# Conditioning in 32-column groups of TensorE, and the sample tokens' convolution as products on GpSimd

## The chip, the cores and the metric

The kernel runs on one core of one Trainium2 chip. The time is that of one execution on the device, in microseconds (us). A core has TensorE (PE, matrix products into PSUM; PEld is its loading of weights), VectorE (DVE), ScalarE (ACT), GpSimd (POOL), SyncE (SP, which here issues every DMA), 16 DMA engines, SBUF with 128 partitions as working memory, and PSUM with eight banks of 128 x 512 f32.

## The reference

One layer of a streaming encoder for two groups of requests with the same weights: a prompt of 1024 tokens and 8 samples of 16 tokens, 1152 tokens of width 1024. All is f32.

```python
sh1, sc1, gt1, sh2, sc2, gt2, sh3, sc3, gt3 = split(silu(c) @ w_ada + b_ada, 9)   # 9 rows c: prompt, 8 samples
x = x + 0.5 * gt1 * swiglu(rms(x) * (1 + sc1) + sh1, w_up1, w_down1)              # first FFN, 2816 wide
z = (rms(x) * (1 + sc2) + sh2) @ w_in            # q, k, v, forget logits, and a pair a, gt for the convolution
o = forgetting_attention(q, k, v, logf)          # 8 heads of 64; samples also see 256 cached rows
u = a * sigmoid(gt)                              # 512 channels, 30 earlier rows in front of each sequence
y = silu(layernorm(depthwise_conv31(u) + conv_b))
x = x + gt2 * (concat(o, y) @ w_out)
x = rms(x + 0.5 * gt3 * swiglu(rms(x) * (1 + sc3) + sh3, w_up2, w_down2))         # second FFN
```

The outputs are x of both groups and the new states (k, v, logf, the last 30 rows of u). What matters here: the conditioning, `silu(c) @ w_ada`, is 9 rows by 1024 by 9216 columns (a weight of 36 MB that is read once); and the convolution gives, for each of 512 channels, 1024 prompt tokens and 8 x 16 sample tokens, a sum of 31 products.

## The kernel before, in words

The 1152 tokens stand in SBUF transposed, in three chunks of 384 columns (c = 0, 1, 2; the samples are the last 128 columns of chunk 2). Large products are made from fp32r parts: each operand is split into hi and lo, and three fp32r matmuls (hi by hi, hi by lo, lo by hi: `mm3`, L478 to L480) stand for one f32 product. Weights come in blocks of 512 KB (`raw`); ScalarE casts them to hi (`wh`, L117) and GpSimd subtracts lo (`wl`, L118), four blocks deep.

The order of TensorE's instructions is that of the program (a manual schedule up to the attention). The other engines' instructions are placed by a scheduler with its own estimates. Work that is woven into TensorE's stream hangs on ticks: `defer(n, f)` runs f at the n-th tick from now, and each half of an up-projection (24 matmuls) and each half of a down-projection ticks once.

The conditioning is cut into 18 groups j of 512 columns, with 8 blocks k of 128 rows each. The first two groups (scale and shift of the first half of the first norm) are full f32 matmuls with 9 columns of stationary data (L348). The others are split: `ahi` on ScalarE (L335), `alo` on VectorE or GpSimd (L336), and two fp32r matmuls (L351, L352) whose 18 stationary columns hold the hi and lo parts of silu(c). Groups 1 and 2 stand ahead of the first FFN, groups 3 and 4 within its first unit, at once; the other 14 are woven into the first FFN, one block a tick (two blocks a tick for the first 20 or so). At a group's end `ada_tail` copies the sum (`ev`), transposes it in four pieces (`pt`), adds the bias into `mods` and makes what the norms and gates use. The blocks of the first four groups come by two loads of 256 KB (`araw`) and one of 1.5 MB (`abulk`) each, the others by one load of 256 KB a block with three buffers.

After the first FFN comes the projection: first the columns of the convolution's pair (`glu`, four tiles ct of 128 channels; `ua` and `ub`), then six column blocks cb of q, k, v (`z`, L872 to L874), nine token tiles each. The convolution runs on VectorE beside it (`conv_taps`): for each ct and each of 31 taps j one operation over 1024 prompt tokens, summed in PSUM (`cv`, L728), and one over the 128 sample tokens, summed in SBUF (`acc`, L729). `run(conv, n)` issues n taps. The attention follows; its first loads (`kp` and others) go into memory that the projection frees. Then the output projection, the second FFN and the final norm.

Of the kernel before, what the change touches and what calls it, by code (L numbers as in the profile page):

```python
# [1 line left out]

# [6 lines left out]
F32 = mybir.dt.float32  # L9
# [34 lines left out]
def trunk_layer(  # L44
# [84 lines left out]
    def kpn(ap):  # L129
        return ap.rearrange("(k p) n -> p k n", p=P)  # L130
# [56 lines left out]
    cst = const.tile([P, KD, 18], F32R, name="cst")  # L187
# [31 lines left out]
    cst32 = pro.tile([P, KD, 9], F32, tag="cst32", name="cst32")  # L219
    xin = {}  # L220

    def load_x(i):
# [78 lines left out]
    KORD = [6, 7, 0, 1, 2, 3, 4, 5]  # L301

    def ada_load(n):
        if n < 18 * KD and n not in ada_raw:
            j, k = ADA_ORDER[n // KD], KORD[n % KD]
            t = adp.tile([P, 512], F32, tag="araw", name="araw", bufs=3)
            sp.dma_start(t, w_ada[0, k * P:(k + 1) * P, j * 512:(j + 1) * 512])
            ada_raw[n] = t

    def ada_bulk(g, tag):  # L310
        j = ADA_ORDER[g]
        for n in range(g * KD, g * KD + 2):
            ada_load(n)
        t = hp.tile([P, 6, 512], F32, tag=tag, name="abulk")
        sp.dma_start(t, kpn(w_ada[0, :6 * P, j * 512:(j + 1) * 512]))
        for k in range(6):
            ada_raw[g * KD + 2 + k] = t[:, k]

    FULL = 2
    NA = 18 * KD  # L320
    ada_q, ada_t, ada_n, ada_p = [], [], [0], [None]

    def ada_split():
        n = ada_n[0]
        ada_n[0] += 1
        if n >= 4 * KD - 2:
            for q in range(max(n, 4 * KD), n + 3):
                ada_load(q)
        raw = ada_raw.pop(n)
        if n < FULL * KD:  # L330
            ada_q.append((n, raw, None))
            return
# [6 lines left out]
    def ada_mm():  # L339
        n, hi, lo = ada_q.pop(0)  # L340
        j, k = ADA_ORDER[n // KD], KORD[n % KD]
        first, last = n % KD == 0, n % KD == KD - 1
        if first:
            ada_p[0] = bank("pa")
        pa = ada_p[0]
        if lo is None:
            r = 9
            pe.matmul(pa[:r, :], lhsT=cst32[:, k, :], rhs=hi, start=first, stop=last)  # L348
        else:
            r = 18  # L350
            pe.matmul(pa[:r, :], lhsT=cst[:, k, :], rhs=hi, start=first, stop=False)  # L351
            pe.matmul(pa[:r, :], lhsT=cst[:, k, :], rhs=lo, start=False, stop=last)  # L352
        if last:
            ev = tmp(512, "ev", r)
            act.copy(ev, pa[:r, :])
            ada_t.append((j, r, ev))

    def ada_tail():
        j, r, ev = ada_t.pop(0)
# [3 lines left out]
        ptv = pt[:, :4 * r].rearrange("p (i s) -> p i s", s=r)  # L363
        dst = mods[:, 4 * j:4 * j + 4, :]
        dve.tensor_tensor(
            dst, ptv[:, :, 0:9], bada[:, 4 * j:4 * j + 4].unsqueeze(2).to_broadcast([P, 4, 9]), ALU.add)
        if r == 18:
            dve.tensor_tensor(dst, ptv[:, :, 9:18], dst, ALU.add)
        finish_mod(j)

    def ada_step():
        if ada_t:
            ada_tail()
        if ada_n[0] < NA:
            ada_split()
            if len(ada_q) > 2:
                ada_mm()
        elif ada_q:
            ada_mm()
        return ada_n[0] < NA or ada_q or ada_t  # L380

    def ada_blocks(n):
        for _ in range(n):
            ada_split()
            if len(ada_q) > 1:
                ada_mm()

    def ada_close():
        while ada_q:
            ada_mm()  # L390
        ada_tail()

    def ada_group():
        ada_blocks(KD)
        while ada_q:
            ada_mm()

    def run(gen, n):
# [204 lines left out]
    ada_tail()  # L603
    ada_group()
    stats_c(0)
    ada_tail()
    ws.split(2)
    ada_bulk(2, "hh2")
    ada_bulk(3, "hl2")
    ws.limit = b_out  # L610

    def chain(c, i):
# [8 lines left out]
    def first(k):  # L621
        if k == 0:
            norm_apply(0, 0, (0, 1))
        elif k == 1:
            for i in range(3, 6):
                place_x(i, xin[i])
        elif k == 4:
            ada_blocks(KD + 2)
            ada_tail()
            ada_blocks(KD - 2)  # L630
            ada_close()
# [84 lines left out]

    def conv_taps():
        for ct in range(4):
            av = acc[ct][:, SEQ:].rearrange("p (s t) -> p s t", t=TS)
            cv = ps.tile([P, SEQ], F32, tag="cv", name="cv", bufs=1)  # L720
            for j in range(CW):
                w = cw[:, ct, j:j + 1]
                u0, u1 = u[ct][:, j:j + SEQ], usv[ct][:, :, j:j + TS]
                if j == 0:
                    dve.tensor_scalar(cv, u0, w, convb[:, ct:ct + 1], ALU.mult, ALU.add)
                    dve.tensor_scalar(av, u1, w, convb[:, ct:ct + 1], ALU.mult, ALU.add)
                else:
                    dve.scalar_tensor_tensor(cv if j < CW - 1 else acc[ct][:, :SEQ], u0, w, cv, ALU.mult, ALU.add)  # L728
                    dve.scalar_tensor_tensor(av, u1, w, av, ALU.mult, ALU.add)  # L729
                yield  # L730

    conv = conv_taps()

    def glu(ct, c, w0, w1):
        pa, pb = glu_mm(c, w0, w1)
# [125 lines left out]
    for cb, (c0, n) in enumerate(QKV):  # L861
# [3 lines left out]
        for tt in [8] + list(range(8)):  # L865
# [18 lines left out]
            else:  # L884
# [30 lines left out]

# [474 lines left out]
```

## Time and profile before

| | us |
|---|---|
| median of 3 runs | 2399.08 (2397.36 to 2401.82) |
| the profiled execution | 2399.03 |
| its span, first to last instruction | 2397.3 |
| PE busy in the span | 2335.4 (97%) |
| DVE busy | 1277.2 (53%) |
| ACT busy | 729.5 (30%) |
| POOL busy | 680.8 (28%) |
| granted TensorE clock, mean | 0.989 |

A row of the page's groups gives line, engine, operation, the tiles written and read, shapes and count; then the busy time, the mean of one in ns, and the idle time of the engine ahead of it with what ended it. A row of the timeline gives the start in us from the span's start, the duration, and the instructions that are merged in it (x4). Matmuls overlap and their ends are modelled, so what one costs is read from start to start. An f32 matmul leaves two records, one for each pass.

### The profile page before, as it was taken

What the parts mean: (1) busy time and instruction counts of PE and PEld (TensorE: products, weight loads), DVE (VectorE), ACT (ScalarE), POOL (GpSimd) and SP (SyncE); (2) the same over time, 40 slices, a digit from 0 to 9 for tenths busy, and PEclk for the clock granted to TensorE, in tenths of its full rate; (3) what the DMA queues carried; (4) which work ended last, traced back from release to release, by engine and by line L of the source; (5) the groups of instructions that cost most, each with busy time, mean ns of one, the idle gap of its engine ahead of it and who ended that gap; (6) DMA issues with size and microseconds to landing.
All of it is one profiled execution on the core that took longest, in us unless ns stands there. A gap on an engine that the chain in (4) does not pass through costs nothing.

```text
span 2397.3 us, 34979 instructions
## 1 busy us (share of the span) xinstructions
PE 2335.4 (97%) x13971; PEld 2236.0 (93%) x13971; DVE 1277.2 (53%) x2381; ACT 729.5 (30%) x1567; POOL 680.8 (28%) x535
## 2 busy tenths in 40 slices
PE   8899999999999999999989999999999999999998
PEld 4899999999999999999987779999999999999997
DVE  5542543343344436799978887744442344333345
ACT  5533222222111113412658764431111111111112
POOL 2254444443211211131536651112112121121220
PEclk9899999999999999999999999999999999999999
DMA  8133333332111111114233331111111111111102
GB/s 296 57 115 96 95 94 99 93 89 66 45 44 36 47 42 36 37 54 140 89 94 126 93 96 36 45 36 51 38 36 53 36 45 44 36 53 36 37 26 79
DMA packets 176699, 165.81 MB, mean 69 GB/s; under 512 B 11135, under 2 KB 143147, under 8 KB 176529
## 3 DMA queue, kind: packets, MB, share of 16 engines
q1 hardware_dynamic: 176537, 163.58, 22.5%
q8 instruction: 110, 1.80, 0.3%
q14 instruction: 52, 0.43, 0.1%
HBM read 147.10 MB, written 16.68 MB: 68 GB/s over the span
## 4 chain that ended last, share of the span: by engine, by line
PE 84%; DVE 10%; ACT 2%; DMA 2%; issue 1%; POOL 0%; SPq 0%; DVEq 0%; ACTq 0%; POOLq 0%
PE ub L479 8%; PE ub L478 8%; PE ub L480 8%; PE ua L479 8%; PE ua L480 8%; PE ua L478 8%; PE d L480 8%; PE d L478 8%; PE d L479 8%; DVE cv L728 4%; DVE acc L729 1%; DMA nfb<-nfd 1%; PE pa L351 1%; PE pa L352 1%; PE wo L480 1%
## 5 line engine op out<-in xcount | busy, mean ns | idle before, releaser
L118 POOL TENSOR_TENSOR wl<-raw,wh 128x1024 fp32r<-128x1024 f32 (+1 forms) x152 | 368.5, 2432 | 1246.3 <-ACT wh L117 1237.9
L517 DVE TENSOR_TENSOR g<-ub,sg 128x384 f32<-128x384 f32 x132 | 73.6, 558 | 764.5 <-PE ub L480 735.8
L478 PE MATMUL ub<-hh,wh 128*128 128x384 f32 x1168 | 397.7, 341 | 2.5 <-ACT hh L462 2.5
L479 PE MATMUL ub<-hl,wh 128*128 128x384 f32 x1168 | 397.5, 340 | 1.9 <-DVE hl L463 1.9
L480 PE MATMUL ub<-hh,wl 128*128 128x384 f32 x1168 | 397.0, 340 | 0.0
L478 PE MATMUL ua<-hh,wh 128*128 128x384 f32 x1136 | 382.0, 336 | 3.7 <-ACT hh L473 3.3
L479 PE MATMUL ua<-hl,wh 128*128 128x384 f32 x1136 | 381.7, 336 | 0.2
L480 PE MATMUL ua<-hh,wl 128*128 128x384 f32 x1136 | 381.3, 336 | 0.0
L485 DVE SCALAR_TENSOR_TENSOR x<-d,hgate,x 128x384 f32<-128x384 f32 (+1 forms) x528 | 296.1, 571 | 134.0 <-PE d L480 127.9
L117 ACT CAST wh<-raw 128x1024 fp32r<-128x1024 f32 (+1 forms) x160 | 165.6, 1050 | 652.4 <-issue 332.6
L478 PE MATMUL d<-gh,wh 128*128 128x384 f32 x1056 | 357.7, 339 | 3.7 <-DVE t L461 3.6
L480 PE MATMUL d<-gh,wl 128*128 128x384 f32 x1056 | 358.1, 339 | 0.0
L479 PE MATMUL d<-gl,wh 128*128 128x384 f32 x1056 | 357.3, 338 | 0.0
L478 PEld LDWEIGHTS ub<-hh,wh 128*128 128x128 f32 x1168 | 221.2, 189 | 7.6 <-ACT hh L462 2.7
L479 PEld LDWEIGHTS ub<-hl,wh 128*128 128x128 f32 x1168 | 221.2, 189 | 4.3 <-DVE hl L463 2.7
L478 PEld LDWEIGHTS ua<-hh,wh 128*128 128x128 f32 x1136 | 214.4, 189 | 9.5 <-ACT hh L473 4.4
L480 PEld LDWEIGHTS ub<-hh,wl 128*128 128x128 f32 x1168 | 221.2, 189 | 0.0
L479 PEld LDWEIGHTS ua<-hl,wh 128*128 128x128 f32 x1136 | 214.3, 189 | 2.9 <-DVE hl L474 1.0
L336 POOL TENSOR_TENSOR alo<-araw,ahi 128x512 fp32r<-128x512 f32 x112 | 149.0, 1335 | 237.2 <-ACT ahi L335 237.2
L480 PEld LDWEIGHTS ua<-hh,wl 128*128 128x128 f32 x1136 | 214.4, 189 | 0.0
L478 PEld LDWEIGHTS d<-gh,wh 128*128 128x128 f32 x1056 | 199.4, 189 | 8.8 <-DVE t L461 3.9
L521 DVE TENSOR_TENSOR gl<-g,gh 128x384 fp32r<-128x384 f32 x132 | 164.6, 1247 | 68.8 <-ACT gh L520 68.8
(274 smaller groups left out, 3634.8 us busy)
## 6 DMA issues: line engine op xcount, KB each, us to landing
raw<-in_w_up_dram SPq DMA_DIRECT2D x88, 512.0 KB
araw<-in_w_ada_dram SPq DMA_DIRECT2D x120, 256.0 KB
raw<-in_w_down_dram SPq DMA_DIRECT2D x44, 512.0 KB
raw<-in_w_in_dram SPq DMA_DIRECT2D x18, 512.0 KB
abulk<-in_w_ada_dram SPq DMA_DIRECT2D x4, 1536.0 KB
out_dram<-yo SPq DMA_DIRECT2D x18, 256.0 KB
out_dram<-qkv SPq DMA_DIRECT2D x34, 128.0 KB
room<-in_cache_k_dram SPq DMA_DIRECT2D x8, 512.0 KB
```

What stands on the lines that cost most here:

```text
L117: act.copy(hi[:, :a * b], raw)
L118: self.sub.tensor_sub(lo[:, :a * b], raw, r32(hi[:, :a * b]))
L336: (pool_e if n >= 4 * KD else dve).tensor_sub(lo, raw, r32(hi))
L351: pe.matmul(pa[:r, :], lhsT=cst[:, k, :], rhs=hi, start=first, stop=False)
L352: pe.matmul(pa[:r, :], lhsT=cst[:, k, :], rhs=lo, start=False, stop=last)
L478: pe.matmul(out, lhsT=wh, rhs=mh_, start=first, stop=False)
L479: pe.matmul(out, lhsT=wh, rhs=ml_, start=False, stop=False)
L480: pe.matmul(out, lhsT=wl, rhs=mh_, start=False, stop=last)
L485: dve.scalar_tensor_tensor(xs[:, :n], b[:, :n], gate[:, dt, 0:1], xs[:, :n], ALU.mult, ALU.add)
L517: dve.tensor_tensor(g32, pb[:, :C], sg, ALU.mult)
L521: dve.tensor_sub(gl[:, cs], g32, r32(gh[:, cs]))
L728: dve.scalar_tensor_tensor(cv if j < CW - 1 else acc[ct][:, :SEQ], u0, w, cv, ALU.mult, ALU.add)
```

## The change

Conditioning. The 18 groups are put into six sets, three of two groups and three of four. silu(c) stands in `cst32`, 9 columns padded with zeros to 32. For each block k of a set, one f32 matmul for each of its groups goes to partitions 32i to 32i + 31 of one PSUM bank `pa` that is kept for it (the rotating banks are seven instead of eight). Splits and their buffers are gone. Blocks of the later sets come as 128 x 2048 (or 128 x 1024) tiles with two buffers; each load is asked for behind the step two earlier. Set 1 stands ahead of the first FFN, set 2 in its first unit; the third set has a step a tick, the others a step every fourth tick. One tail serves a set.

Convolution. `conv_taps` does the prompt tokens alone. `conv_sample` makes, for a channel tile and two samples, all 2 x 16 x 31 products in one GpSimd operation that reads overlapping windows of u and the 31 taps, into a stretch of `acc[3]`, and VectorE sums each 31 in one operation; the bias is added by GpSimd. The one buffer `wn` is shared by all 16 rounds.

```diff
-    nb = 8
+    nb = 7
...
-    act.copy(cst[:, :, 0:9], pcv)
-    dve.tensor_copy(cst32, pcv)
-    dve.tensor_sub(cst[:, :, 9:18], pcv, r32(cst[:, :, 0:9]))
+    dve.memset(cst32, 0.0)
+    dve.tensor_copy(cst32[:, :, 0:9], pcv)
...
-    ADA_ORDER = [2, 0, 3, 1, 4, 5] + list(range(6, 18))
+    SETS = [[2, 0], [3, 1], [4, 5]] + [list(range(j, j + 4)) for j in range(6, 18, 4)]
+    KORD = [6, 7, 0, 1, 2, 3, 4, 5]
+    STEPS = [(s, k) for s in range(len(SETS)) for k in KORD]
...
+        t = adp.tile([P, 2048], F32, tag="araw", name="araw", bufs=2)
+        rows = w_ada[0, k * P:(k + 1) * P]
+        if js == list(range(js[0], js[0] + len(js))):
+            sp.dma_start(t[:, :512 * len(js)], rows[:, 512 * js[0]:512 * (js[-1] + 1)])
+        else:
+            for i, j in enumerate(js):
+                sp.dma_start(t[:, 512 * i:512 * (i + 1)], rows[:, 512 * j:512 * (j + 1)])
...
-        hi = adp.tile([P, 512], F32R, tag="ahi", name="ahi", bufs=3)
-        lo = adp.tile([P, 512], F32R, tag="alo", name="alo", bufs=3)
-        act.copy(hi, raw)
-        (pool_e if n >= 4 * KD else dve).tensor_sub(lo, raw, r32(hi))
-        ada_q.append((n, hi, lo))
...
     def ada_mm():
...
         if first:
-            ada_p[0] = bank("pa")
+            ada_p[0] = ps.tile([P, 512], F32, tag="pa", name="pa", bufs=1)
         pa = ada_p[0]
-        if lo is None:
-            r = 9
-            pe.matmul(pa[:r, :], lhsT=cst32[:, k, :], rhs=hi, start=first, stop=last)
-        else:
-            r = 18
-            pe.matmul(pa[:r, :], lhsT=cst[:, k, :], rhs=hi, start=first, stop=False)
-            pe.matmul(pa[:r, :], lhsT=cst[:, k, :], rhs=lo, start=False, stop=last)
+        for i, raw in enumerate(ada_raw.pop(n)):
+            pe.matmul(pa[32 * i:32 * i + 32, :], lhsT=cst32[:, k, :], rhs=raw, start=first, stop=last)
+        if n >= 2 * KD - 2:
+            ada_load(n + 2)
         if last:
-            ev = tmp(512, "ev", r)
-            act.copy(ev, pa[:r, :])
-            ada_t.append((j, r, ev))
+            ev = tmp(512, "ev", 32 * len(js))
+            act.copy(ev, pa[:32 * len(js), :])
+            ada_ev.append((js, ev))
...
-    ada_bulk(0, "hh1")
-    ada_bulk(1, "hl1")
+    ada_bulk(0, ("hh1", "hl1"))
...
-    ada_group()
+    for _ in range(2):
+        ada_mm()
     place_vec()
     stats_b(0)
-    ada_tail()
-    ada_group()
+    for _ in range(6):
+        ada_mm()
     stats_c(0)
     ada_tail()
...
     def ada_tick():
-        if 5 * KD <= ada_n[0] < 6 * KD + 4:
-            ada_step()
-        if ada_step():
+        if ada_ev:
+            ada_tail()
+        if ada_n[0] < len(STEPS):
+            ada_mm()
+            defer(1 if ada_n[0] < 3 * KD or ada_n[0] % KD == 0 else 4, ada_tick)
+        elif ada_ev:
             defer(1, ada_tick)
...
-                    dve.scalar_tensor_tensor(av, u1, w, av, ALU.mult, ALU.add)
...
+    def conv_sample():
+        wn = acc[3][:, :2 * TS * CW].rearrange("p (s t j) -> p s t j", s=2, j=CW)
+        for ct in range(4):
+            w = cw[:, ct].unsqueeze(1).unsqueeze(1).to_broadcast([P, 2, TS, CW])
+            av = acc[ct][:, SEQ:].rearrange("p (s t) -> p s t", t=TS)
+            for s0 in range(0, NS, 2):
+                win = usv[ct][:, s0:s0 + 2, 0:TS].unsqueeze(3).to_broadcast([P, 2, TS, CW])
+                win = replace(win, ap=[*win.ap[:3], (1, CW)])
+                pool_e.tensor_tensor(wn, win, w, ALU.mult)
+                yield
+                dve.tensor_reduce(av[:, s0:s0 + 2], wn, AX.X, ALU.add)
+            pool_e.tensor_scalar(acc[ct][:, SEQ:], acc[ct][:, SEQ:], convb[:, ct:ct + 1], None, ALU.add)
...
             run(conv, 1 + tt % 2)
+            if cb > 0 and tt % 2:
+                run(convs, 1)
```

More of the change, by code (lines that the diff above doesn't have):

```diff
@@ L1 @@
 from contextlib import ExitStack
+from dataclasses import replace
 import concourse.bass as bass
@@ L186, in trunk_layer @@
     hgate = const.tile([P, 2, KD, 9], F32, name="hgate")
-    cst = const.tile([P, KD, 18], F32R, name="cst")
     xt = [xp.tile([P, KD, C], F32, name=f"x{c}") for c in range(NC3)]
@@ L213, in trunk_layer @@
     mpro, pro = open_pool("pro", "right")
+    cst32 = adp.tile([P, KD, 32], F32, tag="cst32", name="cst32")
     xrows = [x_prompt[0, i * P:(i + 1) * P, :] for i in range(8)] + [x_sample.rearrange("s t d -> (s t) d")]
@@ L218, in trunk_layer @@
     vrow2 = adp.tile([28, P], F32, tag="vrow2", name="vrow2")
-    cst32 = pro.tile([P, KD, 9], F32, tag="cst32", name="cst32")
     xin = {}
@@ L300, in trunk_layer @@
     ada_raw = {}
-    KORD = [6, 7, 0, 1, 2, 3, 4, 5]
     def ada_load(n):
[L304 to L311, printed above, removed]
+        if n >= len(STEPS) or n in ada_raw:
+            return
+        g, k = STEPS[n]
@@ new lines, in ada_load @@
+        js = SETS[g]
+        t = adp.tile([P, 2048], F32, tag="araw", name="araw", bufs=2)
[5 more added lines that the diff above has]
+                sp.dma_start(t[:, 512 * i:512 * (i + 1)], rows[:, 512 * j:512 * (j + 1)])
+        ada_raw[n] = [t[:, 512 * i:512 * (i + 1)] for i in range(len(js))]
@@ L312, in ada_bulk @@
+    def ada_bulk(g, tags):
         for n in range(g * KD, g * KD + 2):
             ada_load(n)
-        t = hp.tile([P, 6, 512], F32, tag=tag, name="abulk")
-        sp.dma_start(t, kpn(w_ada[0, :6 * P, j * 512:(j + 1) * 512]))
-        for k in range(6):
[L317 to L323, printed above, removed]
+        ts = []
+        for j, tag in zip(SETS[g], tags):
+            t = hp.tile([P, 6, 512], F32, tag=tag, name="abulk")
+            sp.dma_start(t, kpn(w_ada[0, :6 * P, j * 512:(j + 1) * 512]))
+            ts.append(t)
+        for k in range(6):
+            ada_raw[g * KD + 2 + k] = [t[:, k] for t in ts]
@@ L324, in ada_split, with ada_mm @@
+    ada_n, ada_p, ada_ev = [0], [None], []
+    def ada_mm():
         n = ada_n[0]
         ada_n[0] += 1
[L326 to L332, printed above, removed]
-        hi = adp.tile([P, 512], F32R, tag="ahi", name="ahi", bufs=3)
-        lo = adp.tile([P, 512], F32R, tag="alo", name="alo", bufs=3)
-        act.copy(hi, raw)
@@ L336, in ada_split @@
[L336 to L341 removed]
+        g, k = STEPS[n]
+        js = SETS[g]
         first, last = n % KD == 0, n % KD == KD - 1
         if first:
[L344 removed]
+            ada_p[0] = ps.tile([P, 512], F32, tag="pa", name="pa", bufs=1)
         pa = ada_p[0]
[L346 to L352 removed]
+        for i, raw in enumerate(ada_raw.pop(n)):
+            pe.matmul(pa[32 * i:32 * i + 32, :], lhsT=cst32[:, k, :], rhs=raw, start=first, stop=last)
@@ L353, in ada_mm @@
+        if n >= 2 * KD - 2:
+            ada_load(n + 2)
         if last:
-            ev = tmp(512, "ev", r)
-            act.copy(ev, pa[:r, :])
-            ada_t.append((j, r, ev))
+            ev = tmp(512, "ev", 32 * len(js))
+            act.copy(ev, pa[:32 * len(js), :])
+            ada_ev.append((js, ev))
     def ada_tail():
-        j, r, ev = ada_t.pop(0)
+        js, ev = ada_ev.pop(0)
+        r = 32 * len(js)
         pt = bank("pt")
@@ L362, in ada_tail @@
             T(pt[:, i * r:(i + 1) * r], ev[:, i * P:(i + 1) * P])
[L363 to L372, printed above, removed]
-            ada_tail()
[L374 to L391, printed above, removed]
+        for i, j in enumerate(js):
+            ptv = pt[:, :4 * r].rearrange("p (i s) -> p i s", s=r)[:, :, 32 * i:32 * i + 9]
+            dve.tensor_tensor(
+                mods[:, 4 * j:4 * j + 4, :], ptv, bada[:, 4 * j:4 * j + 4].unsqueeze(2).to_broadcast([P, 4, 9]),
+                ALU.add)
+            finish_mod(j)
     def ada_group():
-        ada_blocks(KD)
-        while ada_q:
+        for _ in range(KD):
             ada_mm()
@@ L607, in trunk_layer @@
     ws.split(2)
-    ada_bulk(2, "hh2")
-    ada_bulk(3, "hl2")
+    ada_bulk(1, ("hh2", "hl2"))
     ws.limit = b_out
@@ L627, in first @@
         elif k == 4:
-            ada_blocks(KD + 2)
+            ada_group()
             ada_tail()
-            ada_blocks(KD - 2)
-            ada_close()
             norm_apply(0, 0, (2, 3))
@@ L718, in conv_taps @@
         for ct in range(4):
-            av = acc[ct][:, SEQ:].rearrange("p (s t) -> p s t", t=TS)
             cv = ps.tile([P, SEQ], F32, tag="cv", name="cv", bufs=1)
@@ L722, in conv_taps @@
                 w = cw[:, ct, j:j + 1]
-                u0, u1 = u[ct][:, j:j + SEQ], usv[ct][:, :, j:j + TS]
+                x = u[ct][:, j:j + SEQ]
                 if j == 0:
-                    dve.tensor_scalar(cv, u0, w, convb[:, ct:ct + 1], ALU.mult, ALU.add)
-                    dve.tensor_scalar(av, u1, w, convb[:, ct:ct + 1], ALU.mult, ALU.add)
-                else:
-                    dve.scalar_tensor_tensor(cv if j < CW - 1 else acc[ct][:, :SEQ], u0, w, cv, ALU.mult, ALU.add)
-                    dve.scalar_tensor_tensor(av, u1, w, av, ALU.mult, ALU.add)
+                    dve.tensor_scalar(cv, x, w, convb[:, ct:ct + 1], ALU.mult, ALU.add)
+                else:
+                    dve.scalar_tensor_tensor(cv if j < CW - 1 else acc[ct][:, :SEQ], x, w, cv, ALU.mult, ALU.add)
                 yield
+    def conv_sample():
[10 more added lines that the diff above has]
+            pool_e.tensor_scalar(acc[ct][:, SEQ:], acc[ct][:, SEQ:], convb[:, ct:ct + 1], None, ALU.add)
     conv = conv_taps()
+    convs = conv_sample()
     def glu(ct, c, w0, w1):
@@ L911, in trunk_layer @@
             conv_states()
+    while run(convs, 1):
+        pass
     while run(conv, 1):
```

1 line of the change is left out of this document (removed).

## The prediction

> **What bounds the kernel now.** I read the page first, then busy time by stage, then single rows. The profiled execution took 2399.03 us (span 2397.3 us, 1.7 us around it); the median of the three runs is 2399.08 us (2397.36 to 2401.82), so the sum below is made against 2399.0 us. What one measurement of this kernel can tell from no change is about 0.2%, 4.8 us.
>
> ```profile
> span 2397.3 us, 34979 instructions
> PE 2335.4 (97%) x13971; PEld 2236.0 (93%) x13971; DVE 1277.2 (53%) x2381; ACT 729.5 (30%) x1567; POOL 680.8 (28%) x535
> PE 84%; DVE 10%; ACT 2%; DMA 2%; issue 1%; POOL 0%; SPq 0%; DVEq 0%; ACTq 0%; POOLq 0%
> PE ub L479 8%; PE ub L478 8%; PE ub L480 8%; PE ua L479 8%; PE ua L480 8%; PE ua L478 8%; PE d L480 8%; PE d L478 8%; PE d L479 8%; DVE cv L728 4%; DVE acc L729 1%; DMA nfb<-nfd 1%; PE pa L351 1%; PE pa L352 1%; PE wo L480 1%
> ```
>
> TensorE carries 84% of the chain. The one other large piece is VectorE's convolution (L728, L729: 5%, some 120 us), which the change also touches. The stages:
>
> ```profile
> 0.00:12.00 12.00, 6.44 (x33) 6.00 (x34) 3.14 (x9) 3.94 (x6) 1.08 (x8) 1.00 0.82 291
> 12.00:27.00 15.00, 15.00 (x44) 3.75 (x42) 4.94 (x10) 8.43 (x14) 3.51 (x2) 1.00 1.04 344
> 300.00:600.00 300.00, 300.00 (x1687) 282.38 (x1686) 121.53 (x204) 76.50 (x130) 126.99 (x80) 1.00 0.30 88
> 1050.00:1100.00 50.00, 50.00 (x352) 50.00 (x351) 50.00 (x67) 7.94 (x16) 7.26 (x3) 1.00 0.28 81
> 1200.00:1225.00 25.00, 25.00 (x212) 25.00 (x212) 25.00 (x42) 16.02 (x94) 5.66 (x9) 1.00 0.16 53
> ```
>
> The columns after the stretch and its length are busy us of PE, PEld, DVE, ACT and POOL, then granted clock, DMA share, GB/s. Three regimes: the first 27 us run the DMA engines full (0.82 and 1.04, at 291 and 344 GB/s); the first FFN is TensorE alone, with DMA at 0.30; in the projection both PE and DVE are full, so there the chain alone doesn't say which of them paces.
>
> **Term 1, the stream inside the first FFN.** Of 18 groups of 512 conditioning columns, 14 are woven into the FFN, 8 blocks each. A block is two fp32r matmuls (L351, L352):
>
> ```profile
> 111.89 0.40 PE L351 MATMUL pa<-ahi,cst 128*18 128x512 f32 x1
> 112.13 0.40 PE L352 MATMUL pa<-alo,cst 128*18 128x512 f32 x1
> 112.36 0.34 PE L478 MATMUL ua<-hh,wh 128*128 128x384 f32 x1
> 126.39 0.41 PE L252 MATMUL pt<-ident,ev 18*128 18x18 f32 x4
> 126.73 0.41 PE L351 MATMUL pa<-ahi,cst 128*18 128x512 f32 x1
> ```
>
> Start to start a block costs 112.36 - 111.89 = 0.47 us; 112 blocks, 52.6 us. After each group come four transposes, 0.34 us to the next start and some 0.1 us of entry: 14 x 0.44 = 6.2 us. All of it stands in a full PE, so it is on the path.
>
> On TensorE the change does this at one tick of the FFN. Before (ua, ub: the two halves of an up-projection; pa: the conditioning's sum):
>
> ```order
> L480 MATMUL ub<-hh_861,wl 128x384
> L351 MATMUL pa<-ahi,cst 18x512
> L352 MATMUL pa<-alo,cst 18x512
> L478 MATMUL ua<-hh_861,wh 128x384
> L479 MATMUL ua<-hl_862,wh 128x384
> ```
>
> and now, every fourth tick:
>
> ```order
> L449 MATMUL ub<-hh_512,wl 128x384
> L342 MATMUL pa<-araw,cst_105 32x512 x4
> L447 MATMUL ua<-hh_749,wh 128x384
> L448 MATMUL ua<-hl_750,wh 128x384
> ```
>
> So four groups are computed by four f32 matmuls in one place, each into its own 32 partitions, and the splits (ahi, alo) are gone. The stream now has 8 steps of two matmuls and 24 of four, 32 in all. What is a step worth? Full f32 is dear, and column groups exist in the sample attention:
>
> ```profile
> 13.56 5.32 PE L348 MATMUL pa<-abulk,cst 128*9 128x512 f32 x12
> 18.81 0.29 PE L252 MATMUL pv<-ident,vrow 80*128 80x80 f32 x1
> 1295.84 0.61 PE L252 MATMUL pT<-ident,T 128*128 128x128 f32 x4
> 1296.38 0.67 PE L1054 MATMUL sS<-room,room 128*32 128x272 f32 x8
> 1296.97 0.72 PE L1055 MATMUL sS<-room,room 40*128 40x272 f32 x2
> 34.97 2.78 PE L252 MATMUL xb<-ident,xin 128*128 128x128 f32 x24
> 37.50 0.42 PE L478 MATMUL ub<-hh,wh 128*128 128x384 f32 x1
> ```
>
> Six f32 matmuls leave 12 records, two passes each: (18.81 - 13.56) / 12 = 0.4375 us a pass, 0.875 us a matmul of 512 columns. L1054 is four f32 matmuls of 272 columns (8 records) in four 32-column groups: one after another they would take 8 x 0.232 = 1.86 us, and they take 1296.97 - 1296.38 = 0.59. Two passes alone are 0.465, so the four groups run at once and the switch costs 0.59 - 0.465 = 0.125 at the exit, and about 0.10 at the entry (the four transposes before take 0.54, and the last two rows give (37.50 - 34.97) / 24 = 0.11 for one, 0.44 for four). A step of 512 columns: 0.875 + 0.125 + 0.10 = 1.10 us; 32 steps, 35.2 us. Saved: 52.6 - 35.2 = 17.4. Of the tails 4 are left, at 0.65 each (four wide transposes, 0.54, and the entry): 2.6 instead of 6.2, 3.6 saved. **Term 1 is -21.0 us.** Bounds: with no switch cost -28 us; with twice the switch cost -14 us.
>
> [...]
>
> ScalarE's and GpSimd's split operations also vanish; the FFN waits for neither (PE 300.00 of 300.00), so that is worth nothing here. Each step's 1 MB load asks for one buffer of two, freed by the step two earlier, eight ticks of the FFN before its use, at a DMA share of 0.30.
>
> **Term 2, the first two sets, ahead of the FFN and in its first unit.**
>
> ```profile
> 11.69 1.88 PE L348 MATMUL pa<-araw,cst 128*9 128x512 f32 x4
> 26.94 0.44 PE L444 MATMUL rb<-rh,onesr 128*128 128x384 f32 x1
> 29.08 0.45 PE L478 MATMUL ub<-hh,wh 128*128 128x384 f32 x1 [0.93 <-ACT hh L462]
> 5.31 7.76 SPq L307 DMA_DIRECT2D araw<-in_w_ada_dram  x2
> 13.12 0.43 SPq L315 DMA_DIRECT2D abulk<-in_w_ada_dram  x1
> 41.78 0.40 PE L351 MATMUL pa<-ahi,cst 128*18 128x512 f32 x1
> 52.42 0.42 PE L252 MATMUL pt<-ident,ev 18*128 18x18 f32 x4 [0.66 <-ACT ev L355]
> 54.41 0.44 PE L478 MATMUL ub<-hh,wh 128*128 128x384 f32 x1 [1.56 <-ACT hh L462]
> ```
>
> Groups 1 and 2 hold PE from 11.69 to 26.94, with 32 passes; as pairs they have 16, about 7 us, but the third step needs both 1.5 MB loads. Up to them 5.85 MB are asked for: 12 us x 291 GB/s = 3.5 MB, the other 2.35 MB at 344 GB/s take 6.9 us, so 18.9 us. (Before, the second load was issued at 13.12, behind a load waiting for a buffer; now it isn't.) Six steps of 0.875, an entry and an exit end at 24.4; from there to the first ub it was 29.08 - 26.94 = 2.1 us, to which I add an estimated 0.9 for the scale half, whose additions ran ahead before. First ub near 27.4: -1.6 us (0 if the loads land at 20.5, -3.5 if at 17). Groups 3 and 4 stood from 41.78 to 54.41, 12.6 us; now eight steps and an entry are 7.1, the wait for the copy ev 0.7 (0.66 in the row of pt) and pt to ub 2.0 (54.41 - 52.42): 9.8 us. -2.8 us (0 if their loads are late, -4 at best). **Term 2 is -4.4 us.**
>
> **Term 3, the sample tokens' convolution.**
>
> ```profile
> L118 POOL TENSOR_TENSOR wl<-raw,wh 128x1024 fp32r<-128x1024 f32 (+1 forms) x152 | 368.5, 2432 | 1246.3 <-ACT wh L117 1237.9 <-PE pa L352 8.4
> L728 DVE SCALAR_TENSOR_TENSOR cv<-u,cw,cv 128x1024 f32<-128x1024 f32 x116 | 148.4, 1279 | 0.0
> L729 DVE SCALAR_TENSOR_TENSOR acc<-u,cw,acc 128x128 f32<-128x128 f32 x120 | 53.6, 457 | 0.0
> 1200.00:1228.00 28.00, 28.00 (x234) 27.69 (x234) 0.41 (x1) 14.93 (x91) 1.00 0.14 48
> 1229.00:1239.00 10.00, 10.00 (x85) 9.87 (x83) 2.55 (x6) 4.95 (x32) 1.00 0.26 84
> PE kT L252 <- DMA kp<-kd: 2.7, 1, 2.7
> PE cs L252 <- ACT us L760: 2.2, 2, 1.4
> ```
>
> VectorE loses L729, 53.6 us, and gains 16 sums of 992 elements; at L728's rate (1279 ns for 1024) 1.24 us each, 20 us: 34 us less. Is that on the path? The last two stage rows (of the tile z alone) stand on both sides of the conv's end at 1228: 28.00 / 234 = 0.120 us a matmul while VectorE is full, 10.00 / 85 = 0.118 when it is not. TensorE paces itself; VectorE's relief is hidden behind it. The attention then starts on a load (kp) that waits for the projection's end, not for VectorE. What can go is part of the 2.2 us at cs, whose copies lag behind VectorE. **Term 3 is -1 us**, bounds -5 and +6.
>
> GpSimd gains 16 products of 992: nearest row L118, 2432 ns for 1024, so 2.4 us each, 38 us, in a stage where it is nearly idle (7.26 of 50). But they are queued among the weight splits (wl) that TensorE waits for, and share one buffer with the sums, so a product costs 2.4 + 1.3. In GpSimd's queue:
>
> ```order
> L119 TENSOR_TENSOR wl<-raw,wh 128x1024
> L709 TENSOR_SCALAR acc_7425<-acc_7425,vecs 128x128
> L706 TENSOR_TENSOR acc_7428<-u_7422,cw 128x992 x4
> L709 TENSOR_SCALAR acc_7426<-acc_7426,vecs 128x128
> L119 TENSOR_TENSOR wl<-raw,wh 128x1056 x2
> L706 TENSOR_TENSOR acc_7428<-u_7423,cw 128x992 x4
> ```
>
> Before, the two 1056-wide splits (the projection's first weights) followed other splits directly:
>
> ```order
> L118 TENSOR_TENSOR wl<-raw,wh 128x1024 x5
> L118 TENSOR_TENSOR wl<-raw,wh 128x1056 x2
> L118 TENSOR_TENSOR wl<-raw,wh 128x1024 x4
> ```
>
> Now eight products stand ahead of them.
>
> ```profile
> 1046.92 2.48 POOL L118 TENSOR_TENSOR wl<-raw,wh 128x1056 fp32r<-128x1056 f32 x1 [18.58 <-ACT wh L117]
> L741 DVE TENSOR_TENSOR u<-ua,sg x4: 276/276/280, 1020.4 to 1083.2; 128x128 f32<-128x128 f32 x4
> L872 PE MATMUL z<-wh,hh x432: 278/282/457, 1075.1 to 1238.6; 128*128 128x256 f32 x120, 128*128 128x264 f32 x24
> ```
>
> The first sample columns of u exist at 1020.4, the projection starts at 1075.1: 55 us for eight products (8 x 3.7 = 30) and four splits (10). There is room up to 5.7 us a round, a product of 4.4 us.
>
> **Sum:** -21.0 - 4.4 - 1 = -26.4, so 2399.0 - 26.4 = 2372.6, **2373 us**.
>
> **Rivals.**
> - *The groups don't run at once.* A step of four would be 4 x 0.875 + 0.225 = 3.7 us, 24 of them 89, and 8 of two at 1.98, 16: 105 us for 52.6, with the first sets no shorter: about 2450 us, slower. L1054 speaks against it (0.59, not 1.86). 4%.
> - *GpSimd's products hold up the weights (slower than before).* They read overlapping windows, which no row has. From 4.4 us a product on, each further us costs 8 us ahead of the projection; at 7.6 us the 26 us are used up, at 9 us the time is near 2410. For it: no row of that pattern. Against: it needs over three times L118's rate. 4% for slower; 8% for a part, 5 to 6 us a product, near 2382.
> - *No switch price:* 2399 - 28 - 4.4 - 1 = 2366. The 0.125 and 0.10 at L1054 speak against it. 12%.
> - *The start stays bound by DMA:* term 2 is nothing, 2377. For it the shares of 0.82 and 1.04. 17%.
> - *No measurable change*, mishaps cancelling term 1: 3%.
>
> The forecast itself has 52%. **Range:** both bounds of term 1 and the partial GpSimd case give 2362 to 2386. Faster is all but the first, the slower GpSimd case and the cancelling, 0.89; same 0.03; slower 0.08.
>
> **What would show it.** Right: four pa matmuls starting within some 20 ns, and about 1.1 us from the FFN matmul before a step to the one behind it; the first ub near 27.4; no ahi or alo; z still at 0.12 us. Wrong: starts 0.44 us apart within one pass (serial groups); L706 far over 2.4 us with PE idle on wl; the first ub still near 29 behind an abulk load.

## The result, and the profile after

The changed kernel takes 2384.6 us (median; 2384.2 to 2386.2), the kernel before 2398.2 us: a ratio of 0.9943, 95% interval 0.9926 to 0.996. It is faster by 14 us, 0.6%; 26 us were forecast. The head of its page:

```profile
span 2384.4 us, 34134 instructions
PE 2306.2 (97%) x13923; PEld 2210.6 (93%) x13923; DVE 1221.0 (51%) x2241; ACT 653.8 (27%) x1426; POOL 566.2 (24%) x443
PE 86%; DVE 7%; DMA 2%; POOL 2%; ACT 2%; issue 1%; SPq 0%; DVEq 0%; ACTq 0%; POOLq 0%
```

VectorE's share of the chain fell from 10% to 7%, but DVE's busy time only by 56 us, and GpSimd, which was not on the chain, now has 2% of it. Where the time went shows in the first and last starts of three stages: the projection (z), the attention (its first kT to the first wo), and the rest. Of the kernel before (by tile; the first z, 1075.1, stands in the prediction):

```profile
L874 PE MATMUL z<-wh,hl x432: 278/282/420, 1075.3 to 1238.8; 128*128 128x256 f32 x120, 128*128 128x264 f32 x24
L252 PE MATMUL kT<-ident,kp x64: 270/272/423, 1245.0 to 1392.1; 128*64 128x128 f32 x64
L478 PE MATMUL wo<-oth,wh x96: 334/336/634, 1426.8 to 1484.7; 128*128 128x384 f32 x96
```

and of the changed one:

```profile
L852 PE MATMUL z<-wh,hh x432: 277/282/562, 1046.2 to 1218.5; 128*128 128x256 f32 x120, 128*128 128x264 f32 x24
L854 PE MATMUL z<-wh,hl x432: 277/283/415, 1046.4 to 1218.8; 128*128 128x256 f32 x120, 128*128 128x264 f32 x24
L252 PE MATMUL kT<-ident,kp x64: 270/272/421, 1225.0 to 1379.8; 128*64 128x128 f32 x64
L447 PE MATMUL wo<-oth,wh x96: 332/336/636, 1414.8 to 1471.1; 128*128 128x384 f32 x96
```

The ledger: the projection starts 28.9 us earlier (1075.1 to 1046.2), which is more than the conditioning's 25.4 in the forecast. It then lasts 172.6 us instead of 163.7, so 8.9 us are given back. From kT to wo the attention lasts 189.8 us instead of 181.8: 8.0 more are given back, in a stage that the change does not touch. The rest is 0.9 us shorter. -28.9 + 8.9 + 8.0 - 0.9 = -12.9, the difference of the two spans.

### The profile page after: what moved, and what is told of

It reads as the page before. It is cut to its first block, busy times and chain, and to the rows that moved or that the text cites. A ratio compares the mean times of both kernels' runs of the same rounds, so it can differ in the third digit from the quotient of the medians.

```text
span 2384.4 us, 34134 instructions
## 1 busy us (share of the span) xinstructions
PE 2306.2 (97%) x13923; PEld 2210.6 (93%) x13923; DVE 1221.0 (51%) x2241; ACT 653.8 (27%) x1426; POOL 566.2 (24%) x443
## 4 chain that ended last, share of the span: by engine, by line
PE 86%; DVE 7%; DMA 2%; POOL 2%; ACT 2%; issue 1%; SPq 0%; DVEq 0%; ACTq 0%; POOLq 0%
PE ub L447 8%; PE ub L448 8%; PE ub L449 8%; PE ua L447 8%; PE ua L449 8%; PE ua L448 8%; PE d L447 8%; PE d L449 8%; PE d L448 8%; PE pa L342 2%; PE z L852 2%; PE z L854 2%; DMA nfb<-nfd 2%; PE z L853 2%; DVE cv L695 2%; POOL acc L706 1%
## 5 line engine op out<-in xcount | busy, mean ns | idle before, releaser
L119 POOL TENSOR_TENSOR wl<-raw,wh 128x1024 fp32r<-128x1024 f32 (+1 forms) x152 | 365.2, 2410 | 1539.2 <-ACT wh L118 1491.3
L448 PEld LDWEIGHTS d<-gl,wh 128*128 128x128 f32 x1056 | 198.9, 188 | 0.0
L449 PEld LDWEIGHTS d<-gh,wl 128*128 128x128 f32 x1056 | 198.9, 188 | 0.0
```

The lines of the kernel that those rows point to most:

```text
L119: self.sub.tensor_sub(lo[:, :a * b], raw, r32(hi[:, :a * b]))
L448: pe.matmul(out, lhsT=wh, rhs=ml_, start=False, stop=False)
L449: pe.matmul(out, lhsT=wl, rhs=mh_, start=False, stop=last)
```

## The experiments

**Each half alone.** The first kernel has the changed conditioning with the old convolution, the second the old conditioning with the new convolution.

```diff
 cond_only, against the changed kernel
...
-                    dve.scalar_tensor_tensor(cv if j < CW - 1 else acc[ct][:, :SEQ], x, w, cv, ALU.mult, ALU.add)
+                    dve.scalar_tensor_tensor(cv if j < CW - 1 else acc[ct][:, :SEQ], u0, w, cv, ALU.mult, ALU.add)
+                    dve.scalar_tensor_tensor(av, u1, w, av, ALU.mult, ALU.add)
...
-            if cb > 0 and tt % 2:
-                run(convs, 1)
```

> The conditioning in groups, with the sample tokens' convolution as before (128 taps of 128 columns on VectorE). In the two profiles the change's first half had TensorE 27.1 us ahead at the end of the first projection block (before the copies to cs: 1107.2 us against 1080.1), then 7.7 us were lost at cs (TensorE waits 8.75 + 1.76 us there, 1.04 + 1.76 before), and 8.0 us in the attention (first kT to first wo: 181.8 us before, 189.8 after). Theory A (the convolution's sums make VectorE late at cs, the attention's loss is a matter of when one load lands and not of either part): the wait at cs is back under 3 us; time 2371 if the attention takes 182 us, 2379 if it takes 190. Rival B (the time of the conditioning itself falls short, and cs is late for another reason): cs still waits some 9 us, time 2379 to 2385. Rival C (the attention is longer because it begins earlier): cs under 3 us, attention 190 us, time 2379 in every run.

> The conditioning as before, the sample tokens' convolution as products on GpSimd and sums on VectorE. Theory A: the wait at cs rises from 2.8 to about 10.5 us, nothing else moves: 2398.2 + 7.7 = 2406, slower than before; the attention takes what its loads make of it. Rival B: cs waits under 3 us and the time is 2397 to 2398 (the term of -1 us that was predicted). Rival D (the attention's 8 us come with the new convolution): 2406 + 8 = 2414, and the attention takes 190 us here and 182 us with the conditioning alone.

The conditioning alone: 2375.0 us against 2400.6 for the kernel before on that chip, ratio 0.9896 (0.9883 to 0.991). The convolution alone: 2408.6 us, ratio 1.0032 (1.0021 to 1.0044). So the two halves have opposite signs, -25.6 and +8.0; together -17.6, against -13.6 for the change, which the intervals allow. What TensorE waits for in the projection, with the convolution alone:

```profile
PE cs L253 <- ACT us L772: 9.8, 2, 8.5
PE z L884 <- DVE u L753: 1.5, 1, 1.5
```

and with the conditioning alone:

```profile
PE cs L252 <- ACT us L729: 2.2, 2, 1.4
```

Theory A holds for the wait: the long one at cs comes with the new convolution and goes with it. Its guess on the attention, that the loss belongs to neither half, does not hold. The attention took 190.5 us with the conditioning alone and 182.2 with the convolution alone. So its 8 us belong to the conditioning half (rival D is out), and the 2375 us are made of some 30 us gained ahead of the projection and 8 us lost in the attention.

**Why cs waits.** The changed kernel's timeline at that place, where TensorE stands for 8.48 us:

```profile
1088.14 0.16 DVE L861 TENSOR_TENSOR fl<-z,bfb 128x8 f32<-128x8 f32 x1
...
1088.34 0.26 ACT L773 ACTIVATE ezq<-fl 128x72 f32<-128x72 f32 x1 [12.72 <-DVE fl L861]
1088.51 0.28 ACT L740 COPY us<-u 128x128 f32<-128x128 f32 x1
...
1088.84 0.47 PE L252 MATMUL cs<-ident,us 128*128 128x128 f32 x1 [8.48 <-ACT us L740]
```

Read backwards: cs waits for a copy (us), the copy stands behind ezq in ScalarE's queue, ezq waits 12.7 us for the ninth fl, and fl stands in VectorE's queue. VectorE is 8.5 us behind TensorE, which started the last matmul of the ninth tile at 1079.64. Its timeline a little earlier shows why:

```profile
1035.17 1.19 DVE L708 TENSOR_REDUCE acc<-acc 128x32 f32<-128x992 f32 x1 [1.17 <-POOL acc L706]
1036.27 1.28 DVE L695 SCALAR_TENSOR_TENSOR cv<-u,cw,cv 128x1024 f32<-128x1024 f32 x1
1038.67 1.19 DVE L708 TENSOR_REDUCE acc<-acc 128x32 f32<-128x992 f32 x1 [1.12 <-POOL acc L706]
```

and GpSimd's, beside it:

```profile
1032.95 2.19 POOL L706 TENSOR_TENSOR acc<-u,cw 128x992 f32<-128x992 f32 x1 [5.90 <-DVE u L721]
1036.44 2.20 POOL L706 TENSOR_TENSOR acc<-u,cw 128x992 f32<-128x992 f32 x1 [1.30 <-DVE acc L708]
```

A product takes 2.19 us, and with one buffer it starts only when its predecessor is summed. A round takes 3.5 us, in which VectorE does a sum (1.10 from start to start) and a tap (1.28) and stands for the remaining 1.1 us. All 16 rounds are ahead of the ninth fl: the last L708 starts at 1075.2. Two alterations tell apart what of this counts. One moves the copies ahead of ezq on ScalarE, the other gives the products two buffers.

```diff
 us_first
+            conv_states()
             log_sigmoid()
-            conv_states()
 two_buf
-        wn = acc[3][:, :2 * TS * CW].rearrange("p (s t j) -> p s t j", s=2, j=CW)
+        wns = [acc[i][:, :2 * TS * CW].rearrange("p (s t j) -> p s t j", s=2, j=CW) for i in (3, 2)]
...
+                wn = wns[s0 // 2 % 2]
 two_buf_ok, beside that
-            if cb > 0 and tt % 2:
+            if tt % 2:
```

> The changed kernel, with the four copies that cs waits for (us) ahead of the forget gate's exponentials (ezq) on ScalarE; no other engine's order changes. The copies need only u, the exponentials need the last fl, which stands in VectorE's queue behind convolution taps and sums. Theory A (cs waits for the copies, the copies for ezq, and ezq for the late VectorE): the wait of 8.75 + 1.76 us at cs goes almost wholly, VectorE is as late as it was and the rest of the projection (135 us of TensorE) covers that: 2384.6 - 9 = 2375 to 2376. Rival E (VectorE paces the whole projection, and a wait taken away at cs comes back at the next block): TensorE waits in the projection's later blocks and the time stays at 2383 to 2385.

> The changed kernel, with two buffers for GpSimd's products in turn instead of one (acc[3] and acc[2]). With one buffer a product, its sum and the two hand-overs follow each other, and VectorE waits 16.7 us in all, 13 times, for L706. Theory A: GpSimd runs ahead, VectorE's waits fall to some 4 us, it is about 12 us earlier at the last fl, and of the 10.5 us at cs 8 go: 2384.6 - 8 = 2377. Rival F (VectorE is late because the sixteen sums of 1.1 us all stand ahead of the last fl, not because of the waits): the waits fall but cs still waits 6 us or more, 2382.

> The changed kernel with two product buffers in turn, and the products spread over the projection's blocks from the first block on, so that the last of them is done before acc[2] takes its own result. With the buffers alone (two_buf, whose last products fell on top of that result) the time was 2370.8 us against 2384.6, and the projection from first to last z took 160.1 us instead of 172.6. Theory A (VectorE's 16.7 us of waits for single-buffered products set the projection's length): 2370 to 2372 and a projection of 160 to 161 us here too. Rival: two_buf was short because its products or sums went wrong with the data; then this one comes back to 2376 or more.

us_first: 2382.8 us, ratio 0.993 (0.9917 to 0.9942), which can't be told from the changed kernel. The wait at cs went and others took its place:

```profile
PE z L852 <- DVE fl L861: 3.3, 1, 3.3
PE q8T L252 <- POOL kts L881: 1.5, 1, 1.5
PE cs L252 <- DVE fl L861: 1.5, 1, 1.5
...
PE z L852 <- DVE rr L870: 0.8, 1, 0.8
```

fl has to read z out of its bank before the bank can be filled again, and kts and qts wait for rr, which is VectorE's too. Rival E was right: with VectorE 8 us behind, TensorE is held somewhere. The queue on ScalarE was the place of the wait and not its cause.

two_buf: 2370.8 us, ratio 0.9875 (0.9862 to 0.9889). Its last product falls on finished columns of acc[2], so part of the prompt's convolution comes out changed; the operations are the same in number and size, and the projection lasts 160.1 us. two_buf_ok, without that flaw: 2370.3 us, ratio 0.9884 (0.987 to 0.9898), 14.3 us faster than the change, where 8 were expected of two_buf. What VectorE waits for, in the changed kernel from 985 us to 1245 us:

```profile
DVE acc L708 <- POOL acc L706: 16.7, 13, 2.3
```

and in two_buf_ok, 985 us to 1216 us:

```profile
DVE acc L709 <- POOL acc L707: 6.0, 4, 2.3
```

The projection lasts 160.5 us there, 12.1 less than in the changed kernel and 3.2 less than in the kernel before (163.7). All 16 sums still stand ahead of the ninth fl, which now comes 30.6 us behind the first z instead of 42.0. So the shared buffer, not GpSimd's speed, cost the second half of the change its gain; rival F, the sums alone, is out.

**The attention.** VectorE's wait for the bias row of each head, in the kernel before:

```profile
DVE T L1178 <- DMA nfb<-nfd: 3.6, 5, 1.2
```

and in the changed one:

```profile
DVE T L1162 <- DMA nfb<-nfd: 9.0, 7, 2.7
```

nfb has one buffer: a head's load is issued when the head before has read it for the last time, and the first scores wait for it. From the issue to the last of its 4096-byte packets it takes 38.7 us over the eight heads in the profile before and 43.2 in the one after. The loads around it stand in the same order in SP's queue, and the other engines carry out the same operations in the same order through the whole attention. Three kernels ask why, and one takes the load off the path: it loads the first 256 columns, which the first two score blocks need, half a head ahead into a buffer of their own.

```diff
 same_addr
+    gap = const.tile([P, KD, 18], F32, name="gap")
...
+    dve.memset(gap, 0.0)
 nfb_early
+    def n_early(h):
+        nfe[h] = ap_.tile([P, 256], F32, tag="nfe", name="nfe", bufs=1)
+        sp.dma_start(nfe[h], nfd[h:h + 1, :256].to_broadcast([P, 256]))
...
+            elif n % 4 == 2 and h + 1 < H:
+                n_early(h + 1)
...
-        dve.tensor_tensor_reduce(t, s[:, :nk], nfb[h][:, :nk], -1.0, 3e38, ALU.add, ALU.min, st[:, 1:2])
+        dve.tensor_tensor_reduce(t, s[:, :nk], (nfe if i < 2 else nfb)[h][:, :nk], -1.0, 3e38, ALU.add, ALU.min, st[:, 1:2])
```

> The changed kernel with 576 bytes per partition set aside where the dropped constants (cst) stood, so that every buffer of the attention has the address it had before the change; nothing reads them. The attention took 181.8 and 182.2 us in the two profiles with the old conditioning, and 186.7 to 190.5 in the four with the new one; the load nfb lands 38.7 and 40.0 us after its issue there (sum over eight heads), 42.8 to 43.6 here. Theory G (the load lands later because its target has another address): attention 182 us, nfb 39 to 40 us, time 2384.6 - 7 = 2377.5. Rival H (it lands later because of what the DMA queues have done before, or of the time at which the attention begins): attention 187 to 190 us, time 2383 to 2386.

> The kernel before, unaltered, for a second profile of it. Both profiles with the old conditioning have an attention of 182 us (181.8 and 182.2) and nfb landing 38.7 and 40.0 us after its issue (sum of eight), the eight with the new one 184.9 to 190.6 us and 40.0 to 43.6 us, whatever else was altered in them, their addresses included. If the attention's length belongs to the kernel (theory H, what the queues have done before), it is within 0.5 us of 182 again; if it is a matter of the single execution, it may lie anywhere from 182 to 190.

> The changed kernel, unaltered, for a second profile of it. Theory H: an attention within 1 us of the 189.8 of its first profile. If it is a matter of the single execution: another value between 184 and 191, and then the 8 us lost there are not a property of the change, though all ten profiles together say that the old conditioning fares better by 3 to 8 us.

> The changed kernel, with the first 256 columns of each head's bias row (nfb) loaded a second time into a small buffer of their own, half a head ahead; only the two first score blocks of a head read it, so that the large load has one more stage of the head to land. 1 MB more is moved in all. Theory A (the attention's length hangs on nfb, for which the first scores of each head wait 9.0 us on VectorE and 9.6 us on TensorE in the profile): these waits fall under 2 us, the halved clock behind some of them goes too, and the attention takes 176 to 180 us instead of 189.8: 2384.6 - 11 = 2374. Rival (the wait moves to the next stage of the head, or to kp): attention 186 us or more, 2381 to 2385.

same_addr: 2385.1 us, ratio 0.9942 (0.9928 to 0.9955), attention 186.3 us. The old addresses do not bring the old length back; the 3.5 us that are missing from 189.8 lie within the spread below. before_again: 182.5 us in the attention; after_again: 189.8, as in the first profile. So the length belongs to the program and not to the execution, as far as one repeat of each can show. Over all profiles with the one nfb load it was 181.8, 182.2 and 182.5 with the old conditioning and 184.9 to 190.6 in nine with the new one. nfb_early: 2377.5 us, ratio 0.9908 (0.9895 to 0.9922), attention 179.8 us, 7 us faster than the change (11 were expected). The waits for the load that are left:

```profile
DVE T L1166 <- DMA nfb<-nfd: 3.8, 2, 2.0
```

With the load off the path the 8 us are gone: they hang on it. (The early load was not tried on the kernel before, so how much of its gain would come there too isn't known.) Why the load lands later after the new conditioning is not shown: addresses alone are not the reason, and what the queues have carried before (80 fewer transfers, some of 1 MB) and the earlier start of the attention remain guesses.

Part of the 8 us is the clock. The changed kernel's stretches around its longest wait for nfb (2.4 us of TensorE; the columns are as in the prediction, the clock is the third figure from the end):

```profile
1272.00:1274.30 2.30, 0.00 (x0) 0.00 (x0) 0.29 (x3) 0.00 (x0) 0.70 (x1) 1.00 0.82 234
1275.00:1277.40 2.40, 2.40 (x14) 2.27 (x13) 2.22 (x9) 1.78 (x6) 0.85 (x2) 0.50 0.00 0
1279.00:1281.00 2.00, 2.00 (x19) 0.99 (x17) 1.44 (x3) 1.42 (x3) 0.98 (x4) 1.00 0.00 0
```

Such a piece at 0.50 behind a wait for nfb stands twice in each of the two profiles of the changed kernel, and in none of the kernel before, of nfb_early or of joined. The attention's length goes with their number: none in the three profiles with the old conditioning (181.8 to 182.5 us), and with the new one a single piece at 184.9 to 186.7 us (four profiles), two at 188.2 to 189.8 (three), three at 190.5 and 190.6. In the first profile of the kernel before no wait for nfb exceeds 1.2 us (the last figure of its row).

**The price of a visit, and the start.**

```diff
 pairs
...
             ada_mm()
-            defer(1 if ada_n[0] < 3 * KD or ada_n[0] % KD == 0 else 4, ada_tick)
+            if ada_n[0] > 3 * KD:
+                ada_mm()
+            defer(1 if ada_n[0] <= 3 * KD or ada_n[0] % KD == 0 else 8, ada_tick)
 filler
     place_vec()
+    fb = bank("fill")
+    for _ in range(16):
+        pe.matmul(fb[:, :P], lhsT=ones, rhs=ident, start=True, stop=True)
```

> The changed kernel with the 24 late steps of the conditioning done two at a time, every eight ticks of the FFN instead of one every four: the same matmuls in 12 visits instead of 24. A visit of one step costs 1.20 us in the trace: 0.474 from the first to the last start, 0.522 to the next FFN matmul, 0.094 more than usual ahead of it and 0.106 more for the FFN matmul behind it. Theory A (0.09 + 0.09 + 0.11 us are paid for each entry and exit, not for each step): a visit of two steps costs 1.20 + 0.87 = 2.07 us, 12 x 0.33 = 4 us saved, 2380 to 2381. Rival (each step pays, or a load of 1 MB is late now that two are used at once): 2.4 us a visit or waits on araw, 2384 or more.

> The changed kernel with 16 matmuls of 128 columns, on constants and into a bank that nobody reads, in the 3.9 us in which TensorE waits for the first chunk's sums (13.9 to 17.8 us). After that wait the first 3.8 us of the conditioning's matmuls run at a granted clock of 0.55, starts 0.43 us apart where a pair of column groups takes 0.43 for both. Theory A (the drop follows the idle time): clock 1.00 from 18.6 us on, six steps in 5.2 us instead of 6.8, the first ub at 27.4 instead of 28.98. Rival (the drop follows the switch to column groups, or the loads are late): clock near 0.55 and first ub near 29 as before.

A visit of one step in the changed kernel (timeline of PE):

```profile
141.73 0.34 PE L449 MATMUL ub<-hh,wl 128*128 128x384 f32 x1
142.00 1.07 PE L342 MATMUL pa<-araw,cst 128*32 128x512 f32 x8
142.99 0.44 PE L447 MATMUL ua<-hh,wh 128*128 128x384 f32 x1
143.27 0.34 PE L448 MATMUL ua<-hl,wh 128*128 128x384 f32 x1
```

and one of two steps in pairs:

```profile
189.00 0.34 PE L449 MATMUL ua<-hh,wl 128*128 128x384 f32 x1
189.27 1.92 PE L342 MATMUL pa<-araw,cst 128*32 128x512 f32 x16
191.12 0.44 PE L447 MATMUL ub<-hh,wh 128*128 128x384 f32 x1
191.40 0.34 PE L448 MATMUL ub<-hl,wh 128*128 128x384 f32 x1
```

From the FFN matmul before to the second one behind there are 1.54 us, of which the two FFN matmuls would take 0.35: 1.19 us. With two steps 2.40 - 0.35 = 2.05, as theory A has it: the 0.3 us are paid per visit. In pairs the projection starts at 1042.4, 3.8 us earlier (in the nine profiles with single steps, at 1043.8 to 1048.2). The time is 2376.2 us, ratio 0.9906 (0.9893 to 0.992), 8.4 less than the change. The attention makes up the difference: it took 184.9 us here, which the pairs themselves do not explain.

At the start, the changed kernel's stretches from 13.9 us on:

```profile
13.90:17.80 3.90, 0.17 (x1) 0.02 (x1) 3.43 (x4) 2.96 (x5) 0.00 (x0) 1.00 1.04 388
18.58:22.38 3.80, 3.80 (x10) 1.36 (x11) 1.11 (x4) 2.29 (x5) 0.45 (x1) 0.55 1.20 310
22.38:25.90 3.52, 3.52 (x17) 1.15 (x13) 0.00 (x0) 1.04 (x1) 3.52 (x2) 1.00 1.01 394
```

and the second of these with the filler:

```profile
18.58:22.38 3.80, 3.13 (x16) 0.94 (x18) 0.94 (x3) 1.64 (x4) 0.20 (x1) 1.00 1.20 310
```

The idle 3.9 us cost the clock, as theory A says: 0.55, and 10 starts in a stretch that has 1.00 and 16 with the filler. But the first ub came only from 28.98 to 28.26, not to 27.4 (the other profiles with the new conditioning have it between 28.5 and 29.8), because the matmuls, now faster, caught up with the loads:

```profile
19.25 1.05 PE L342 MATMUL pa<-abulk,cst 128*32 128x512 f32 x4 [0.69 <-DMA abulk<-in_w_ada_dram]
```

From 30.1 us on 6.8 us at a clock of 0.50 followed with the filler, where the changed kernel has 3.4 us of it. The projection started at 1047.6, no earlier, and the whole took 2383.9 us in its one run.

**All three together.** two_buf_ok, pairs and nfb_early in one kernel.

> The changed kernel with the three alterations that gained, together: two product buffers (14.3 us in the medians), late steps of the conditioning in pairs (8.4 us, of which 3.8 us stand at the start of the projection), and the small early bias load. Each acts in a stage of its own, so the gains add: 2384.6 - 14.3 - 3.8 - 11 = 2355 to 2356 if the early load brings its 11 us, 2366 if it brings nothing. Rival (VectorE or GpSimd, freed in one stage, is the bound of the next): 2370, no better than the two buffers alone.

joined: 2362.1 us (2357.5 to 2363.7), ratio 0.9845 (0.9832 to 0.9859): 37.7 us faster than the kernel before. Its profiled execution had a span of 2355.8 us, with a projection of 159.8 and an attention of 179.9 us. The sum of the gains that were measured singly is 14.3 + 3.8 + 7.1 = 25.2, that is 2359.4: they add within 3 us, and no freed engine became the next bound.

## Why the prediction was right, and where its terms were off

The direction and the mechanism of the main term were right, and the time lies in the range; the likeliest value was 12 us too low. That it lies inside is in part luck: the 17 us lost in the projection and the attention stood in no term, and the range had room for them because it allowed for mishaps that did not come. By its own steps:

- **Term 1, right in kind, the step mis-sized.** The groups do run at once: the four pa matmuls of a pass start 7 ns apart, and the second pass 0.43 us behind the fourth. A step costs 1.19 us instead of 1.10. The FFN matmul behind it starts its successor 0.28 us later where 0.17 is usual, and this 0.1 us was not in the sum: 32 x 0.09 = 3 us. The stream so saves 18 us, not 21. Within the first FFN the traces show more, because the two streams stand at different places in it. From the 301st FFN matmul to the 3001st, before and after (of the tile pa alone; the columns behind the length are busy us of PE, PEld and ACT, clock, DMA share and GB/s):

```profile
124.20:651.45 527.25, 64.39 (x208) 18.96 (x208) 7.43 (x13) 1.00 0.30 87
126.80:626.61 499.81, 24.50 (x184) 3.62 (x184) 1.76 (x3) 1.00 0.26 85
```

  27.4 us are gained there, and as much in two other pairs of profiles (before_again and after_again, conv_only and cond_only). But the stretch holds 104 of the 112 old blocks (208 matmuls) and all 14 tails, against 23 of the 32 new steps (184 records) and 3 of the 4 tails; the other nine steps stand between the second chunk's statistics and the stretch, where some 3 to 5.5 us are lost. 1.8 of the 27.4 us are FFN matmuls that start 174.3 ns apart instead of 175.0, which no row explains. At the projection's start the gain was 28.9, 33.2 and 31.1 us in the three pairs; what varies lies outside the stretch, where TensorE waits and the clock drops to 0.50.
- **Term 2, half right.** The second set was forecast at -2.8 us, and the next statistics came 2.9 us earlier. The first set brought 0.1 us instead of 1.6. The estimate of the loads was right (18.9 us; the matmuls started at 18.58), but the six steps from there took 7.3 us, to the next matmul at 25.91, where the forecast had them end at 24.4; the granted clock was 0.55 in the first 3.8 us. Fewer matmuls left TensorE idle for 3.9 us, where before the change it was busy from 11.69 to 26.94. The step took the pass at full rate for granted.
- **Term 3, wrong in sign: -1 us forecast, +8.0 measured** on the convolution alone, outside its bounds of -5 and +6 (the interval, 5.0 to 10.6 us, reaches into them; in its profile the projection is 9.4 us longer). GpSimd was not the reason: 2.19 us for a product, where 2.4 was forecast, and no weight came late. Three steps failed. First, L729 was taken at its mean of 457 ns; in the stage 104 of the 120 take some 0.26 us from start to start (1034.23 to 1034.49 below), so VectorE was relieved of some 31 us, not 54 (an estimate: the other 16 stretch to as much as 2.3 us). Second, the sums' waits for the products were counted in GpSimd's time ("a product costs 2.4 + 1.3") but not in VectorE's, whose queue stands still with them: 16.7 us. With 16 sums of 1.10, 17.6, that is 34 us, so nothing was relieved. Third, the place: before, 56 of the 120 sample taps stood ahead of the ninth fl and the others later, beside TensorE's work; now all of it stands ahead. There was no slack at that place: cs waited 2.2 us for it already.

```profile
1033.04 1.28 DVE L728 SCALAR_TENSOR_TENSOR cv<-u,cw,cv 128x1024 f32<-128x1024 f32 x1
1034.23 0.35 DVE L729 SCALAR_TENSOR_TENSOR acc<-u,cw,acc 128x128 f32<-128x128 f32 x1
1034.49 1.28 DVE L728 SCALAR_TENSOR_TENSOR cv<-u,cw,cv 128x1024 f32<-128x1024 f32 x1
```

- **"TensorE paces itself" in the projection** was right to 3 us: with the sums out of the way the stage took 160.5 us instead of 163.7.
- **The attention** was held to start as before, only earlier; that it would also last 8 us longer was in no term and no rival.
- **The rivals.** Serial groups, no switch price and slow products are all refuted by the rows above (1.19 us a step, where two passes alone are 0.875 and serial groups 3.5; 2.19 us a product). What "the start stays bound by DMA" forecast, no gain, came true for the first set alone, first through the clock and only behind it through the loads. The time that the partial GpSimd rival gave (2382) came near the measured one for another reason: the round trip cost VectorE's time, not GpSimd's.

## What to carry to other kernels

When work moves to an idle engine and its result comes back, count the round trip in the queue of the engine that takes it back: with one buffer VectorE's queue here stood 16.7 us for the products, with two 6.0, and the second buffer was worth 14 us, more than the move itself. The wait that was taken away where it showed (8.5 us for the copies at cs) came back elsewhere (3.3 us at z, 1.5 each at q8T and cs), as VectorE was late; look for what makes the engine late. Here four small f32 matmuls in column groups took little longer than one (0.99 us to the next start against 0.875), but each visit had a price of 0.3 us of its own, so visit seldom and do much.

## What was not expected of the hardware

- The granted clock drops to 0.50 behind waits of TensorE of some 2 us, which no term of the forecast had. In six profiles (two of either kernel, cond_only and joined) every piece at half rate but the last of a run lasts 3.413 us or a multiple of it; in the first profile of either kernel the records hold the rates 1.00 and 0.50 alone, and the pieces begin a whole number of 3.413 us apart. Laid on that grid, all 65 pieces begin behind a window in which TensorE's records leave 1.5 us or more idle (61 of them 1.7 or more); in those two first profiles it is 23 pieces, 22 of them with 1.7 or more. Of the windows at full rate with 1.4 to 1.9 us idle, 12 were followed by half rate and 13 were not (2 and 3 in the two); with more, all 53 were (21 in the two), except in the first 7 us of a run, where full rate is on record throughout. So some half a window was enough: in the changed kernel 2.00 us idle in the one that ends at 29.16 us, with half rate for 3.413 us behind it. Such a wait costs up to 1.7 us more (half of 3.413 us, an estimate).
- One broadcast load of 512 KB, the same transfer in the same order of its queue, lands 4.8 to 5.0 us after its issue (mean over the heads, three profiles) with the old conditioning in the program, and 5.0 to 5.6 us (nine profiles) with the new (4.8 and 5.4 us in the first profile of either kernel; in the changed one the first is issued 740 us behind the last conditioning load, which is issued at 477.4). A second profile of either kernel gave the same length of the attention within 0.7 us.
- GpSimd multiplies overlapping windows (31 taps, each window one column further) at 2.19 us for 992 products, no dearer than its plain difference of 1024 columns at 2.40 us (L119).
